# RWKV outputs in two sweeps of a bank, and larger steps of attention, scan and filters, in a two-layer encoder

## The chip, the cores and the metric

The kernel runs on one core of one Trainium2 chip. The metric is the device time of one execution in microseconds (us). Three runs of the kernel before took 3458.44, 3468.43 and 3473.36 us; their median is 3468.43.

## What is computed

A trunk of two layers on 1024 tokens with 1024 channels, all in float32. Each layer normalises, mixes tokens, adds, normalises again and applies a SwiGLU block; shifts, scales and gates come from a condition vector. Layer 1 mixes with long convolutions whose filters are computed from positions. Layer 0, where the change lies, mixes with two groups side by side:

```
y_attn = blocked_gqa(q, k, v)                # 8 heads of 64, 2 heads of keys, softmax over all 1024 keys
state = state * w_t + sz * b_t + v_t * k_t   # RWKV-7, 8 heads of 64 x 64, sz = state z_t
y_t   = state r_t                            # one scan forward, one backward, summed
...
return concat(y_attn, groupnorm(y) + bonus, gated) @ w_out
```

The filters of layer 1 depend on weights alone (`hid @ w_out`, a decay window, then a transform), so they can be computed at any time before layer 1.

## The kernel before

**Storage.** SBUF is cut into pages of 128 x 1024 floats and PSUM into its eight banks. Both are handed out and taken back while the program is written down, the oldest free one first. In the mixer's second part the banks are in two groups of four: group 0 for RWKV, group 1 for attention and the filters.

**The work of layer 0's mixer.** First come the projections (`stream`), with the start of the first RWKV unit beside them (`first`). Then comes a loop over the RWKV units, `for i in range(1, len(units) + 2)` in `mixer`. A unit is a direction and a pair of heads; there are eight, and each goes through three stages in three successive turns of the loop:

- `rwkv_x`: decays by a scan (L1214), products inside chunks of 64 tokens (L1263), and inverses of 16 x 16 blocks on VectorE, with trips through DRAM ahead of and behind them.
- `rwkv_y`: products of 64 x 64 blocks that make the inverses of whole chunks (L1327), transposes (L1345), the chunk-level products (L1374, L1383, L1393) and their forms by head (L1410).
- `rwkv_s`: what each chunk adds to the state (L1435), 14 steps from state to state (L1452, each followed by one VectorE operation), then the outputs (L1467, L1470) of 16 chunks in two banks, and for the second direction the group norm (`rwkv_post`).

A turn `i` runs `rwkv_s` of unit i-2, `rwkv_y` of unit i-1 and `rwkv_x` of unit i, and beside them a number of steps of `beside()`: attention first, with three steps of the filters' hidden layer in it, then the filters.

**Attention.** A step handles 128 queries of one head against all keys: `scores` (L924, L925, two banks; maxima L928 and L929; exponentials L932), `turn` for the tile before (L947 transposes into two banks one after the other, L948 copies them out), and after each fourth tile `values` (L964), whose bank is held for two pairs of tiles.

**Filters.** `hy_filters` goes over 16 groups of channels; each has four `t`: taps (L1735, windows by exponentials L1737, product L1738) and their transform (L1749, L1698 to L1700), then an eight-point transform on VectorE (`dft8`, L1648 and L1649).

**What sets the order.** Each stage is a Python generator; a `yield` ends a step. `weave` draws steps from several generators in proportion to a length that is given with each: it always takes the next step of the one that has gone through the smallest share of its length. The lengths are the numbers of steps: 27 for `rwkv_s`, 36 for `rwkv_y`, 16 for `rwkv_x`, and 46 to 50 of `beside()`. The framework's scheduler gets the instructions in that order. It may let an instruction that is ready pass one that is not, by its own estimate of times, and then fixes one order for each engine. Pages and banks are bound before that, in the order of the steps.

**Products on TensorE.** The array is used whole or in parts: a product with 64 rows of contraction takes 64 rows of it, one with 64 outputs takes 64 columns. The profile writes this tile as rows\*columns. The outputs alternate, per chunk, between two products over the 128 rows of `UV` (tile 128\*64) and two over a 64-row state (64\*64). A float32 product appears as two MATMUL instructions, so each chunk and line gives four.

Of the kernel before, what the change touches and what calls it, by code (L numbers as in the profile page):

```python
# [32 lines left out]
def rows(ap):  # L33
    """[n*128] (or [a, n*128]) vector -> [rows, 128]."""
    if len(ap.shape) == 2:
        return ap.rearrange("a (r w) -> (a r) w", w=P)
    return ap.rearrange("(r w) -> r w", w=P)
# [9 lines left out]
def weave(*gens):  # L47
    """Runs generators of steps side by side, in proportion to their lengths: (n, generator). A step counts for what it
    yields, or for one; one that yields "wait" has to wait for the others."""
    live = [[0, n, g] for n, g in gens]  # L50
    while live:
        live.sort(key=lambda x: x[0] / x[1])
        s = live[0]
        try:
            cost = next(s[2])
            if cost != "wait":
                s[0] += cost or 1
            elif len(live) > 1:
                s[0] = s[1] * (live[1][0] / live[1][1] + 1e-6)
        except StopIteration:  # L60
            live.pop(0)
# [7 lines left out]
def some(gen, n):  # L69
    """The next n steps of a generator."""  # L70
    for _ in range(n):
        if next(gen, gen) is gen:
            return
        yield


class Kern:
    """The kernel's shared state and building blocks.

    SBUF is cut into pages and PSUM into banks, handed out and taken back while the program is traced: the oldest  # L80
    free one first, so that reuse waits as little as it can. Pages are for float32 ([128, 1040]) or for float32r
    operands of products ([128, 1024]); repage() cuts the free ones anew between the parts of the program.
    """

# [32 lines left out]
    def fence(self, dt, n=1 << 30, first=0):  # L117
        """Only the pages from `first` up to the n-th are for common use."""
# [11 lines left out]
    def repage(self, nf, nr):  # L130
        """Cuts the pages into nf of float32 and nr of float32r; those in use stay."""
# [36 lines left out]
    def set_banks(self, *counts):  # L168
        """Splits the (free) banks into groups."""
# [23 lines left out]
    def small(self, tag, shape, bufs, dt=F32):  # L193
        """One of `bufs` small tiles in turn; the caller sees to it that an older use has ended by then."""
# [20 lines left out]
    def load_cols(self, spec):  # L215
        """spec: list of (key, AP [rows, width] or tuple of APs set side by side); a row becomes a column. Steps of 128."""
# [42 lines left out]
    def split(self, t, shape=(P, 1024)):  # L259
        """The pair of a page, which is given back."""  # L260
# [5 lines left out]
    def load_w(self, ap, kt, ncol):  # L266
        """ap: DRAM [kt*128, ncol] -> (hi, lo), [128, kt, ncol] each; ap may also be what presplit() returned."""
# [9 lines left out]
    def presplit(self, ap, kt, ncol, name):  # L277
        """The pair of load_w() as DRAM tiles."""
# [7 lines left out]
    def mm3(self, ps, w, mov, first=True, last=True, halves=(0, 1)):  # L286
        """ps[n] = sum_k w[k]^T mov[k][:, n-th half]; pairs (hi, lo) of [128, M] and [128, 1024]. The first and last
        addends may be left to other calls."""
# [9 lines left out]
    def proj_steps(self, w, c0, width, h, g=0, ahead=None, n=4, apart=False):  # L298
        """proj_tile() in n steps; the halves one after the other if `apart`."""
# [15 lines left out]
    def stream(self, w, h, tiles, g=0):  # L315
        """Projections one after another, each one's `post` beside the next: (column, width, post), post(banks) a generator."""
# [19 lines left out]
    def proj_tile(self, w, c0, width, h, g=0, ahead=None):  # L336
        """w[:, c0:c0+width]^T h in two banks; a column in `ahead` is that of the next call, whose weights are loaded here."""
# [33 lines left out]
    def ada_first(self):  # L371
        """Layer 0's first two sixths, by the tensor engine."""
# [19 lines left out]
    def ada_cols(self, layer, part, half, acc, g):  # L392
        """The columns of half a sixth from rows to be summed."""
# [13 lines left out]
    def ada_part(self, layer, part, g=0, lag=0):  # L407
        """Modulation columns of one sixth: [128, 8] at self.mod[:, layer*48 + part*8]. The last product of a half comes
        `lag` steps after its sums."""
# [35 lines left out]
    def rstd(self, acc, n):  # L445
        """1/sqrt(mean_D(x^2) + eps) on all partitions, [128, 512] of a half in PSUM; acc holds sums of squares."""
# [12 lines left out]
    def normed(self, xT, steps, use, lag, keep=None):  # L459
        """use(n, m, r) for the halves n of the tiles m of x, r the bank of rstd(); `steps` yields (n, m) as they get done,  # L460
        half 0 first. A tile that is done goes to the tile `keep` in DRAM. Half 0 is used beside the steps of half 1, from
        its step `lag` on."""
# [31 lines left out]
    def inv_sqrt(self, out, ps, mult, add=None, floor=None):  # L494
        """out = 1/sqrt(ps*mult + add) or 1/sqrt(max(ps, floor))."""
# [8 lines left out]
    def norm_h(self, xT, layer, which, steps, lag, keep=None):  # L504
        """rmsnorm(x)*gain*(1+scale)+shift as pairs of [128 channels, 1024 tokens]; for the rest see normed()."""
# [23 lines left out]
    def head_cols(self, sq, g):  # L529
        """sq [128 = 2 heads x 64, 1024 tokens] -> bank [128 tokens, 8 blocks, 2 heads] of sums."""  # L530
# [5 lines left out]
    def head_bcast(self, cols, n, g):  # L536
        """cols [128 tokens, 8, 2 heads] -> bank [128 = 2 heads x 64, 512] of token half n."""
# [7 lines left out]
    def to_tok(self, out, src, g):  # L545
        """src [128 channels, 1024 tokens] -> out [128 tokens, 8 blocks, 128 channels]."""
# [9 lines left out]
    # The up-projections multiply blocks of 2 x 2 (two tiles of outputs, halves of the channels, halves of the tokens)  # L556
    # with seven products, Winograd's form of Strassen's: with C = A B,
    # S1 = A21 + A22, S2 = S1 - A11, S3 = A11 - A21, S4 = A12 - S2,
    # T1 = B12 - B11, T2 = B22 - T1, T3 = B22 - B12, T4 = T2 - B21,
    # U2 = A11 B11 + S2 T2, U3 = U2 + S3 T3,  # L560
    # C11 = A11 B11 + A12 B21, C12 = U2 + S1 T1 + S4 B22, C21 = U3 - A22 T4, C22 = U3 + S1 T1.

    def ffn(self, xT, before, layer, up=iter(()), down=iter(()), low=None):
        """x, in pages once the steps `before` are done -> pages of x + the FFN's part and the last steps to them; `up` and
        `down` run beside the two halves. These steps use few of the first `low` pages for operands."""
# [62 lines left out]
        # the first pair of tiles: plain products, while the sums are made  # L628
# [38 lines left out]
        def prep():  # L667
            """The left operands, in the order of the products."""
# [72 lines left out]
        # down, the last tiles first  # L741
# [27 lines left out]
    def matvec_add(self, xT, w, ys, layer, part, g=0, keep=None):  # L769
        """x += gate * (w^T y); x is given as pages, or as tiles in DRAM, which are updated or else kept as pages."""  # L770
# [26 lines left out]
    def matvec_halves(self, xT, w, ys, layer, part, low=None):  # L797
        """matvec_add() by halves of the tokens: loads the weights and returns steps that yield (half, tile); ys are given back."""
# [27 lines left out]
    def attn_tiles(self):  # L826
        """Keys, queries and token-major values, kept in DRAM: what becomes of each projection, for stream()."""
# [6 lines left out]
        def normed(gain, keep):  # L834
            """RMSNorm over the head and rotary positions."""
# [46 lines left out]
    def attention(self, out, G):  # L882
        """Softmax attention with queries on partitions; fills out[0..3] with DRAM tiles [128 channels, 1024 tokens]."""
# [5 lines left out]
        def keys(g):  # L889
            """[hi; hi] and [lo; lo] of a group's keys."""  # L890
# [9 lines left out]
        def queries(t):  # L900
            """The queries of a pair of heads: [hi; lo] and [lo; hi]."""
# [8 lines left out]
        def scores(t, qt, e):  # L910
            """Products with all keys, maximum, exponentials and their sum: a page [128 queries, 1024 keys]."""
# [27 lines left out]
        def turn(pr, t, qt, e):  # L939
            """Keys on partitions, two tiles of queries side by side: pages [128 keys, 4 tiles, 256 queries]."""  # L940
            if qt % 2 == 0:
                st["p", e] = [self.page((P, 4, 256)) for _ in range(2)]
            for n in range(2):
# [6 lines left out]
                yield  # L950
            self.free(pr)

        def values(t, qt):
            """Sums of the values, [2 heads x 64, 256 queries up to tile qt]."""
# [7 lines left out]
            for k in range(8):  # L962
                for e in range(2):
                    nc.tensor.matmul(o[H64[e], x : x + 256], v[:, k, H64[g]], pT[e][k // 4][:, k % 4], start=k == 0, stop=k == 7)  # L964
                if k % 2 == 1:
                    yield
            self.free(pT)
            if qt % 4 == 3:
# [12 lines left out]
                yield  # L981
# [7 lines left out]
        for i in range(n + 1):  # L989
            if i < n:  # L990
                exps[i] = scores(*steps[i])
                yield
            if i:
                yield from turn(exps.pop(i - 1), *steps[i - 1])
            if i % 4 == 0 and i:
                yield from values(*steps[i - 1][:2])
        self.free(st["k"], v)

# [30 lines left out]
    def padded(self, ps, width=P):  # L1029
        """Two banks -> page [width, 1026] with a zero before and after; gives the banks back."""  # L1030
# [9 lines left out]
    def mixed(self, pad, j, width=P):  # L1040
        """The centred token shift of projection columns 768 + 128 j.., given padded: page."""
# [9 lines left out]
    def rwkv_tiles(self):  # L1051
        """What becomes of each projection of this part, for stream(): decay rates, in-context rates and output gates of all
        heads; r, k, v, -kk, bonus and token-major v of the pairs of heads; all kept in DRAM."""
# [3 lines left out]
        def rates(key, j, b0, dst):  # L1057
            def post(ps):
# [5 lines left out]
                # a direction's values as [hi; lo] ([lo; hi] for the second); the weights' hi on both halves, lo beside the values' hi  # L1064
# [136 lines left out]
    # A unit is a direction and a pair of heads; c = 2 pr + p is a chunk of 64 tokens, e a head of the pair. In a tile of  # L1201
# [895 lines left out]
def consts():  # L2097
    """Arrays that depend on the shapes alone."""
    f = np.float32
    k = {}  # L2100
# [76 lines left out]
```

## Time and profile before

| what | value |
| --- | --- |
| median of three runs | 3468.43 us |
| span of the profiled execution | 3477.4 us |
| time of the profiled execution itself | not recorded apart from its span |
| instructions | 52810 |
| the mixer's second part (the loop), from 440 to 1345 us | 905 us |
| turns of the loop that hold attention and all three stages | 94 to 108 us each |
| mean granted TensorE clock over the span | 0.956 |

The span runs from the first to the last instruction of one profiled execution. Shares of busy time are shares of that span. Products are pipelined and overlap on TensorE, so the distance from one start to the next says more than their lengths.

### The profile page before, as it was taken

The numbers are of one execution on the slowest core, as the hardware profiler recorded it, in microseconds if no ns is written. First come the engines' busy times: TensorE is split into PE (matmuls) and PEld (weight loads), VectorE is DVE, ScalarE is ACT, GpSimd is POOL, SyncE is SP. The second block draws the span as 40 slices with busy tenths as digits, with TensorE's granted clock in tenths as the row PEclk, the third lists the DMA queues.
The fourth block names the chain that finished last, engine by engine and source line by source line (L and its number), as shares of the span: only waits on it lengthen the run. The fifth ranks groups of instructions, "written<-read, shape, count | busy, mean of one in ns | idle before, by whom it ended". The sixth has DMA issues, their size and how long they took to land.

```text
span 3477.4 us, 52810 instructions
## 1 busy us (share of the span) xinstructions
PE 3277.4 (94%) x20739; PEld 2639.1 (76%) x20739; DVE 2355.9 (68%) x4281; ACT 1255.1 (36%) x2296; POOL 240.6 (7%) x502
## 2 busy tenths in 40 slices
PE   8999989999998998999999999989987799999998
PEld 4577766777677887887788887778876688888887
DVE  5345556566667778587777666589987786667545
ACT  4523245556543543342223333321221153333211
POOL 2000000000011231000000220000000000000000
PEclk9789989999998999999999999999998899999999
DMA  7454523333324326234444994324336523223411
GB/s 261 172 164 148 159 84 75 73 96 82 73 63 105 99 77 213 79 127 151 158 147 135 359 356 160 103 81 144 121 104 228 177 74 108 73 73 129 146 53 49
DMA packets 332536, 458.89 MB, mean 132 GB/s; under 512 B 103992, under 2 KB 234897, under 8 KB 332288
## 3 DMA queue, kind: packets, MB, share of 16 engines
q1 hardware_dynamic: 292576, 321.65, 30.1%
q0 software_dynamic: 39536, 133.81, 11.3%
q8 instruction: 163, 2.67, 0.3%
q14 instruction: 85, 0.70, 0.1%
q10 hardware_dynamic: 176, 0.07, 0.0%
HBM read 311.27 MB, written 141.56 MB: 130 GB/s over the span
## 4 chain that ended last, share of the span: by engine, by line
PE 60%; DVE 9%; DMA 5%; issue 4%; ACT 2%; SPq 0%; POOL 0%; DVEq 0%; ACTq 0%; POOLq 0%
PE bk L296 22%; PE bk L600 7%; PE bk L602 7%; PE bk L601 7%; PE bk L1749 4%; PE bk L1735 2%; PE bk L1770 2%; DMA p<-in_ada_w_dram 2%; DVE p L1648 1%; DVE p L257 1%; PE bk L1263 1%; PE bk L1327 1%; PE bk L947 1%; DMA p<-in_hy_w_in_dram 1%; PE bk L964 1%
## 5 line engine op out<-in xcount | busy, mean ns | idle before, releaser
L296 PE MATMUL bk<-p,p 128*128 128x512 f32 (+1 forms) x5136 | 1252.3, 403 | 66.9 <-ACT p L256 26.4
L296 PEld LDWEIGHTS bk<-p,p 128*128 128x128 f32 (+1 forms) x5136 | 979.5, 193 | 304.4 <-ACT p L256 30.1
L256 ACT ACTIVATE p<-p 128x512 fp32r<-128x512 f32 (+3 forms) x534 | 395.8, 759 | 930.3 <-PE bk L601 260.6
L257 DVE TENSOR_TENSOR p<-p,p 128x512 fp32r<-128x512 f32 (+3 forms) x534 | 443.5, 848 | 225.3 <-ACT p L256 183.6
L601 PE MATMUL bk<-p,p 128*128 128x512 f32 x1248 | 488.3, 392 | 3.8 <-DVE p L257 3.8
L600 PE MATMUL bk<-p,p 128*128 128x512 f32 x1248 | 488.4, 393 | 0.0
L602 PE MATMUL bk<-p,p 128*128 128x512 f32 x1248 | 487.6, 392 | 0.2 <-DVE p L257 0.2
L601 PEld LDWEIGHTS bk<-p,p 128*128 128x128 f32 x1248 | 236.3, 189 | 53.4 <-DVE p L257 4.7
L602 PEld LDWEIGHTS bk<-p,p 128*128 128x128 f32 x1248 | 236.2, 189 | 50.4 <-DVE p L257 0.8
L600 PEld LDWEIGHTS bk<-p,p 128*128 128x128 f32 x1248 | 236.1, 189 | 48.9
L787 DVE SCALAR_TENSOR_TENSOR p<-bk,mod,p 128x512 f32<-128x512 f32 x192 | 135.0, 745 | 119.8 <-PE bk L296 116.6
L1648 DVE TENSOR_TENSOR p<-p 128x128 f32<-128x128 f32 (+2 forms) x544 | 174.0, 383 | 0.0
L429 DVE SCALAR_TENSOR_TENSOR p<-p,cond,p 128x512 f32<-128x512 f32 x140 | 104.5, 748 | 82.7 <-DMA p<-in_ada_w_dram 81.0
L1749 PE MATMUL bk<-p,p 128*128 128x128 f32 x1024 | 137.0, 290 | 2.7 <-DVE p L1700 2.6
L1749 PEld LDWEIGHTS bk<-p,p 128*128 128x128 f32 x1024 | 126.5, 201 | 7.9 <-ACT p L1737 2.4
L928 DVE TENSOR_REDUCE mx<-bk 128x1 f32<-128x512 f32 x128 | 86.9, 685 | 61.8 <-PE bk L925 58.8
L1737 ACT ACTIVATE p<-delta,k_tneg 128x128 f32<-128x128 f32 x256 | 87.9, 394 | 84.0 <-DMA hs<-p 14.0
L1036 ACT COPY p<-bk 128x512 f32<-128x512 f32 (+1 forms) x80 | 44.0, 589 | 197.3 <-DVE p L1797 64.3
L948 ACT COPY p<-bk 128x512 f32<-128x512 f32 x128 | 74.4, 588 | 105.3 <-PE bk L947 100.7
L932 ACT ACTIVATE p<-bk,mx 128x512 f32<-128x512 f32 x128 | 87.0, 686 | 29.4 <-DVE mx L929 29.0
L947 PE MATMUL bk<-k_ident,p 128*128 128x128 f32 x512 | 85.0, 294 | 10.8 <-ACT p L932 9.3
L1327 PEld LDWEIGHTS bk<-p,p 64*64 64x64 f32 x2048 | 73.0, 137 | 28.9 <-issue 17.6
(404 smaller groups left out, 4373.4 us busy)
## 6 DMA issues: line engine op xcount, KB each, us to landing
p<-in_ffn_w_dram SPq DMA_DIRECT2D x120, 512.0 KB, 4.5
p<-in_ada_w_dram SPq DMA_DIRECT2D x96, 512.0 KB, 4.5
sp_f<-p POOLq DMA_DIRECT2D x36, 512.0 KB, 5.5
p<-sp_f POOLq DMA_DIRECT2D x36, 512.0 KB, 5.4
hs<-p POOLq DMA_DIRECT2D x64, 256.0 KB, 3.1
p<-hs SPq DMA_DIRECT2D x32, 512.0 KB, 4.2
p<-sp_r SPq DMA_DIRECT2D x24, 512.0 KB, 5.6
p<-sp_x SPq DMA_DIRECT2D x24, 512.0 KB, 4.5
```

The lines of the kernel that those rows point to most:

```text
L256: self.nc.scalar.activation(out=hi, in_=src, func=AF.Copy)
L257: self.nc.vector.tensor_tensor(out=lo, in0=src, in1=hi.bitcast(F32), op=ALU.subtract)
L296: nc.tensor.matmul(ps[n], a, b[:, HALVES[n]], start=s, stop=e)
L429: nc.vector.scalar_tensor_tensor(out=acc, in0=wt[:, i], scalar=self.cond[:, k : k + 1], in1=acc, op0=ALU.mult, op1=ALU.add)
L600: nc.tensor.matmul(ps, op[:, 0, k], mh, start=start and k == 0, stop=False)
L601: nc.tensor.matmul(ps, op[:, 0, k], ml, start=False, stop=False)
L602: nc.tensor.matmul(ps, op[:, 1, k], mh, start=False, stop=stop and k == 3)
L787: nc.vector.scalar_tensor_tensor(out=xs, in0=ps[n], scalar=self.modc(layer, part, m), in1=xs, op0=ALU.mult, op1=ALU.add)
L947: nc.tensor.transpose(pt[:, j], pr[:, k * P : (k + 1) * P], self.ident)
L1327: nc.tensor.matmul(pt[H[p], pr], lhs(e, pr, p), rhs[H[p], 8 * e + pr], start=True, stop=True)
L1648: tt = lambda o, a, b, op: nc.vector.tensor_tensor(out=o, in0=a, in1=b, op=op)
L1749: nc.tensor.matmul(ps[:, j, ri], F[2 * d + t2 // 4][:, t2 % 4, 128 * ri : 128 * ri + 128], tp[:, j, d], start=d == 0, stop=d == 1)
```

## The change

Two things. First, in `rwkv_s` the outputs of a bank are made in two sweeps: all products with `UV` (the very first of them marked as the start), then all products with the states (the last one marked as the end). Second, many `yield`s go. Attention has one per step, the blocks of `rwkv_y` and `rwkv_x` one per bank, the sums of `rwkv_s` one per bank, and a filter step now holds the transform of `t` with the taps of `t + 1` written ahead of it. The lengths for `weave` are set to the new numbers of steps. `rwkv_x` in `first()` also has 12 steps in place of 16, while its length there stays at 30. Arithmetic, operands, tiles and transfers stay. The diff also takes out comments.

```diff
 def turn(pr, t, qt, e):
                 self.fbank(pt)
-                yield
             self.free(pr)
 def values(t, qt):
-                if k % 2 == 1:
-                    yield
...
                 self.fbank(o, rb)
-                yield
...
             if i < n:
                 exps[i] = scores(*steps[i])
-                yield
             if i:
-                yield from turn(exps.pop(i - 1), *steps[i - 1])
+                turn(exps.pop(i - 1), *steps[i - 1])
             if i % 4 == 0 and i:
-                yield from values(*steps[i - 1][:2])
+                values(*steps[i - 1][:2])
+            yield
 def rwkv_x(self, u, G):
-                if j == 1:
-                    yield
 def rwkv_y(self, u, G):
-                    if pr == 3:
-                        yield
...
                 nc.scalar.copy(BT[i][:, q : q + 4], pt)
                 self.fbank(pt)
-                yield
+            yield
...
             nc.scalar.copy(ZV[:, :, :, 0:64], pt)
             self.fbank(pt)
-            yield
...
-                    if pr == 3:
-                        yield
 def rwkv_s(self, u, ys, out, G):
-                if c == 3:
-                    yield
...
             for j in range(8):
                 c = 8 * i + j
-                only = c == order[0]
                 for e in range(2):
-                    nc.tensor.matmul(pt[H[e], j], UV[i][:, j, e], R[e][:, c], start=True, stop=only)
-                if not only:
-                    for e in range(2):
-                        nc.tensor.matmul(pt[H[e], j], S[H[e], c], RP[H[e], c % 2, c // 2], start=False, stop=True)
-                if j % 2 and j < 7:
-                    yield
+                    nc.tensor.matmul(pt[H[e], j], UV[i][:, j, e], R[e][:, c], start=j == 0, stop=False)
+            later = [j for j in range(8) if 8 * i + j != order[0]]
+            for j in later:
+                c = 8 * i + j
+                for e in range(2):
+                    nc.tensor.matmul(pt[H[e], j], S[H[e], c], RP[H[e], c % 2, c // 2], start=False, stop=j == later[-1])
 def mixer(self, w, h, ada):
-                if n in (210, 230, 250):
+                if n in (50, 55, 60):
                     next(f)
...
-            n = (0, 48, 48, 48, 48, 50, 48, 46, 50, 48)[i]
+            n = (0, 12, 12, 12, 12, 12, 16, 33, 33, 33)[i]
             gens = [(n, some(other, n))]
             if i > 1:
-                gens.append((27, self.rwkv_s(units[i - 2], ys, outr, 0)))
+                gens.append((19, self.rwkv_s(units[i - 2], ys, outr, 0)))
             if i <= len(units):
-                gens.append((36, self.rwkv_y(units[i - 1], 0)))
+                gens.append((20, self.rwkv_y(units[i - 1], 0)))
             if i < len(units):
-                gens.append((16, self.rwkv_x(units[i], 0)))
+                gens.append((12, self.rwkv_x(units[i], 0)))
 def hy_filters(self, g):
-                for t in range(4):
+                def taps(t):
...
-                    yield
+                    return tp
+                nxt = taps(0)
+                for t in range(4):
+                    tp = nxt
+                    if t < 3:
+                        nxt = taps(t + 1)
                     ps = self.bank(g, (P, 2, 2, W))
```

## The prediction

> **What bounds the kernel now.** I read the whole span first, then stretches of it, then the order of TensorE's products inside the stretch that the change touches. The page of the profile gives the span and TensorE's share.
>
> ```profile
> span 3477.4 us, 52810 instructions
> PE 3277.4 (94%) x20739; PEld 2639.1 (76%) x20739; DVE 2355.9 (68%) x4281; ACT 1255.1 (36%) x2296; POOL 240.6 (7%) x502
> PE 60%; DVE 9%; DMA 5%; issue 4%; ACT 2%; SPq 0%; POOL 0%; DVEq 0%; ACTq 0%; POOLq 0%
> ```
>
> The chain that ended last is 60% TensorE. The 3477.4 us are the span of the profiled execution; the three runs without a profile have a median of 3468.43 us, so the profiled execution lies 9 us (0.3%) above it. What I work out are differences, and I take them off the median. A measurement of this kernel can tell about 0.5% (17 us) from no change.
>
> The changed steps lie in one stretch, from 440 to 1345 us. In the view by windows the columns are the length, then the busy time of PE, PEld, DVE, ACT and POOL, the granted clock, DMA share and GB/s.
>
> ```profile
> 440.00:1345.00 905.00, 855.13 (x9870) 683.91 (x9869) 606.03 (x1554) 469.76 (x1133) 99.84 (x168) 0.95 0.34 87
> 836.00:940.00 104.00, 101.85 (x1208) 71.46 (x1208) 72.32 (x157) 63.33 (x135) 3.01 (x6) 1.00 0.38 88
> 1048.00:1165.00 117.00, 105.34 (x1151) 90.44 (x1148) 80.92 (x236) 51.49 (x139) 22.15 (x36) 0.90 0.35 88
> 1258.00:1345.00 87.00, 85.88 (x721) 77.49 (x720) 75.54 (x241) 31.38 (x94) 23.33 (x36) 1.00 0.43 133
> 1345.00:1362.00 17.00, 6.49 (x49) 5.91 (x50) 13.00 (x37) 7.62 (x8) 4.51 (x6) 0.61 0.74 267
> ```
>
> The last four rows are three of the nine turns of the mixer's loop (one unit's start, one unit's middle and one unit's end, beside attention or filters) and what follows. TensorE is busy for 98% of the turn at 836 and for 99% of that at 1258, DVE for 70% and 87%. So here TensorE's own time sets the pace, and I ask what that time consists of. In the timeline of TensorE the columns are start, length to the last end, operation, tile of the array (rows\*columns), shape of the moving operand, and how many products.
>
> ```profile
> 1332.76 3.81 PE L1749 MATMUL bk<-p,p 128*128 128x128 f32 x32 [0.34 <-DVE p L1700]
> 1336.50 0.33 PE L1470 MATMUL bk<-p,p 64*64 64x64 f32 x4
> 1336.76 0.34 PE L1467 MATMUL bk<-p,p 128*64 128x64 f32 x4
> ...
> 1340.19 0.33 PE L1470 MATMUL bk<-p,p 64*64 64x64 f32 x4
> ...
> 1184.01 0.71 PE L1749 MATMUL bk<-p,p 128*128 128x128 f32 x4
> 1184.65 0.33 PE L1452 MATMUL bk<-p,p 64*64 64x64 f32 x4
> 1184.91 0.44 PE L1345 MATMUL bk<-k_ident,p 128*128 128x128 f32 x2
> 1185.28 1.61 PE L1327 MATMUL bk<-p,p 64*64 64x64 f32 x48
> 1186.73 0.28 PE L1452 MATMUL bk<-p,p 64*64 64x64 f32 x4
> 1186.85 0.63 PE L1327 MATMUL bk<-p,p 64*64 64x64 f32 x16
> 1187.41 0.44 PE L1345 MATMUL bk<-k_ident,p 128*128 128x128 f32 x2
> ```
>
> Between 1336.50 and 1340.19 the two lines of the outputs alternate in groups of four, 14 groups in 3.69 us, 0.264 us each. From 1185.28 to 1187.41 there are 68 products of the same 64x64 size, of two lines but of one tile, in 2.13 us. The row in their midst, L1452, costs nothing extra, although it is another line into another bank: 1186.85 - 1186.73 = 0.12 us for four. At 1184.65 the same four products, with 128\*128 ahead and behind, take 0.26. So it is the change of tile that costs: 0.26 - 0.12 = 0.14 us. With that one change taken off, a product in a run is (2.13 - 0.14) / 68 = 0.029 us. A wide tile pays about as much: four of L1749 from 1184.01 to 1184.65 take 0.64 us, against 4 x 3.74 / 32 = 0.47 in the run of 32 at 1332.76. I take 0.14 for every change, with 0.10 and 0.17 as bounds.
>
> How often does it occur? I counted, over the timeline of TensorE from 440 us (first row below) to 1345 (last row), how many products have another tile than the one ahead of them: 950 of 9869. At 0.14 that is 133 of 905 us.
>
> ```profile
> 439.83 0.61 PE L296 MATMUL bk<-p,p 128*128 128x512 f32 x2
> ...
> 1343.20 1.02 PE L1492 MATMUL bk<-p,k_blkones 128*128 128x512 f32 x2
> ```
>
> Does the order come from the code or from the scheduler? I wrote out the turns of `weave` with the tile of each step's products: 959 changes in the order in which the code hands its steps over, against 950 on the chip. By turn of the loop it is 122 to 126 for the second to fifth turn, and the chip has 113 to 143. So the scheduler keeps to the code's order nearly everywhere, and the new order can be written out too.
>
> **The outputs in two sweeps.** The rows of the two lines in the stretch (busy time, mean ns):
>
> ```profile
> L1467 PE MATMUL bk<-p,p 128*64 128x64 f32 x512 | 45.2, 244 | 0.0
> L1470 PE MATMUL bk<-p,p 64*64 64x64 f32 x480 | 41.4, 242 | 0.0
> ```
>
> These 992 products stand in 248 groups of four, 248 x 0.264 = 65.5 us. After, a bank has 32 products of one tile and then 28 to 32 of the other: 992 x 0.029 = 28.8 us, and 16 banks with a change in their middle and mostly one at the end, 32 x 0.14 = 4.5. That is 32 us less. As some groups already ran on into products of the same tile (my list has 242 changes behind these two lines, not 248), I take 31. The flags of the first and last product are not an operation; the number of products, copies and additions stays.
>
> **Larger steps.** A turn of the loop had 48 + 27 + 36 + 16 = 127 steps and has 12 + 19 + 20 + 12 = 63. Attention yields once per tile of queries and no more after scores, each four transposes and each four products of the values; `rwkv_y` and `rwkv_x` yield per bank, no longer per half bank; a filter step holds the products of L1749 and the next L1735. The list of turns, changes behind the products of each part, before and after: attention 208 and 68; `rwkv_y` 238 and 114; `rwkv_x` 56 and 28; states (L1452) 93 and 53; additions to the state (L1435) 24 and 15; filters 90 and 45; the rest 8 and 8. Outside the outputs that is 717 and 331, 386 fewer, x 0.14 = 54 us (39 to 66 by the bounds). In all 85 us.
>
> **What is given back.** First, the four banks of attention. `scores` takes two; `turn` for the tile before takes one after the other; the values hold a fourth for half of the time. With three in the ring the second `turn` gets a bank that `scores` has just filled, and has to wait for its maximum and exponentials. That stood apart by other steps before, and is in one step now. It is so in 32 of the 64 steps, and 8 more times the bank of the values itself is such a one. The length of the wait, with empty queues, is two maxima, the scaling and one exponential:
>
> ```profile
> L928 DVE TENSOR_REDUCE mx<-bk 128x1 f32<-128x512 f32 x128 | 86.9, 685 | 61.8 <-PE bk L925 58.8 <-ACT p L1269 2.5
> L929 DVE TENSOR_SCALAR mx<-mx 128x1 f32<-128x1 f32 x64 | 13.3, 209 | 0.9
> L932 ACT ACTIVATE p<-bk,mx 128x512 f32<-128x512 f32 x128 | 87.0, 686 | 29.4 <-DVE mx L929 29.0
> L947 PE MATMUL bk<-k_ident,p 128*128 128x128 f32 x512 | 85.0, 294 | 10.8 <-ACT p L932 9.3 <-DVE p L979 0.8 <-ACT p L948 0.6
> ```
>
> 2 x 0.685 + 0.209 + 0.686 = 2.3 us, less 0.5 for four transposes that run meanwhile, 1.8 us. Queued behind the waiting transposes on TensorE are the values and whatever RWKV step follows. I expect the scheduler to put RWKV steps of the 4 x 1 us or so that lie between two attention steps into the gap; then each of the 40 costs two changes of tile, 80 x 0.14 = 11 us. The bound on the other side is a rival below.
>
> Second, the turn of the loop gets shorter than one unit's start is long. Its first scan is at 643.63, and the first products that need its result are at 747.51:
>
> ```profile
> 643.63 2.32 DVE L1214 TENSOR_TENSOR_SCAN p<-p,p 128x1040 f32<-128x1040 f32 x1 [1.07 <-DMA p<-sp_w]
> ...
> 747.51 1.15 PE L1327 MATMUL bk<-p,p 64*64 64x64 f32 x32
> ```
>
> 104 us, a turn of the loop as it is now. If turns shorten by 9 us, `rwkv_y` starts that much later in its turn, and only attention and the states can fill. TensorE is not busy for 905 - 855 = 50 us of the stretch now. Between nothing and 9 us for each of eight units lies 0 to 72; most of the 98% busy turns speak for the low end, and I take 15.
>
> Third, the end: from 1345 to 1362 DVE is busy for 13 of 17 us and TensorE for 6.5, so the filters' tail is DVE's already. There the last turn's 41 fewer changes (6 us) buy half: 3 us given back. The taps made one step ahead save a wait that hardly exists, 2.7 and 0.4 us in all (last column), so I cost them at nothing.
>
> ```profile
> L1749 PE MATMUL bk<-p,p 128*128 128x128 f32 x1024 | 137.0, 290 | 2.7 <-DVE p L1700 2.6
> L1735 PE MATMUL bk<-wo,p 128*128 128x256 f32 x256 | 80.1, 446 | 0.4 <-DVE p L1738 0.3
> ```
>
> The start of unit 0, beside the projections, has 12 steps instead of 16 at the same weight, and ends earlier; the wait of L1327 for it is 4.3 us once:
>
> ```profile
> PE bk L1327 <- DMA p<-o: 4.3, 1, 4.3
> ```
>
> That is 0 to 4 us gained; I leave it at nothing. No queue of SP or POOL gets more to do; the loads and stores move along with their steps.
>
> The sum: 31 + 54 - 11 - 15 - 3 = 56 us. 3468 - 56 = 3412 us. With 0.10 and 0.17 per change and 0 to 40 for the unit's start it runs from 3385 to 3438.
>
> **Rivals.** *The scheduler cuts the pieces anew* (the change doesn't do what it says). A step that is not ready is passed by others, and each passing makes changes of tile again. Against it stands 959 against 950. For it, the steps are longer and wait oftener. Then the outputs keep their 31, the other 54 shrink to half, and the losses stay: 3468 - (31 + 27 - 29) = 3439 us.
>
> *DVE and ACT become the bound.* DVE is at 70% of the turn at 836, 69% of that at 1048, and 87% of the last. If it can hold no more than 75%, those turns may shrink to 96, 108 and not at all, where I expect about 95, 108 and 81: some 10 us less gain, 3422 us. The Trainium skill says in "TensorEngine Tiling (Array Packing)", PSUM Bottleneck, that packing speeds up TensorE but not the emptying of PSUM, which may then become the bound; by that the gain would be cut in every turn, and the trace shows room for it in all but the last.
>
> *The unit's start paces the loop.* If a turn cannot get shorter than the 104 us of scan to result, only the two turns without such a start gain: 99 - 40 and 68 - 27 changes, 100 x 0.14 = 14 us, 3454 us, no change that can be told. Against it: L1327 waits for that result once.
>
> *Slower: TensorE waits inside the attention step.* The place is the second `turn` (and the first product of the values), 40 times. If nothing stands in the gap and the queues of DVE and ACT hold other work, a wait is 1.8 us and as much again, 3.6 x 40 = 144 us, against 85 gained; the two other losses (18 us) come on top. 3468 - 85 + 144 + 18 = 3545 at that price; it decides from 40 waits of (85 - 18) / 40 = 1.7 us on, so already the bare 1.8 us with no filling ends at 3473, and 2.5 us at 3501, which I take. For it: one order holds for all engines, and a wait misjudged at compile time stalls everything behind it. Against it: L947 waits 9.3 us for L932 in 512 products now. The Trainium skill, "TensorE: Matmul & The Clock Gate", HAM oscillation, adds that an idle gap above about 3.4 us halves TensorE's clock; the turn at 1048, with 12 us not busy, has 0.90 granted, which agrees.
>
> **How the numbers follow.** Forecast 3412 us, chance 0.60. Pieces cut anew 0.15, DVE and ACT 0.07: both faster by over 0.5%. The unit's start 0.10: within 0.5%. The wait in attention 0.08: slower. So faster 0.82, same 0.10, slower 0.08. The range from 3385 to 3458 takes in the forecast's own, the first three rivals, and leaves out the slower one and the tails, 0.16.
>
> **What would show it.** In the timeline of TensorE after: L1467 and L1470 in runs of 28 to 32, 0.9 to 1.1 us each; 400 to 480 changes of tile in the stretch; the stretch from the first L924 to the last L1749 some 55 us shorter, its turns at 90 to 95 us; TensorE still above 93% busy there, DVE up by 5 points. Wrong would be: over 600 changes (cut anew), L947 waiting for L932 for more than 40 us (the slower rival), L1327 waiting for the reloaded inverse for more than 30 us (the unit's start), or DVE above 85% in the turns with attention.

## The result and the profile after

The changed kernel takes 3483.53 us in the median of 20 runs (3461.60 to 3498.55), the kernel before 3473.53 in as many runs on the same chip (3458.44 to 3482.30). The ratio is 1.0027 [1.0016, 1.0038]: no change that can be told at 0.5%, where I forecast 3412 us. The head of the page of the profiled execution after, then its chain of waits by engine:

```profile
span 3480.2 us, 52831 instructions
PE 3244.6 (93%) x20739; PEld 2630.9 (76%) x20739; DVE 2349.4 (68%) x4281; ACT 1253.5 (36%) x2296; POOL 241.4 (7%) x502
PE 67%; DVE 14%; DMA 9%; issue 5%; ACT 4%; SPq 0%; POOL 0%; DVEq 0%; ACTq 0%; POOLq 0%
```

TensorE is busy 33 us less than before and the span is 3 us longer. So work went away, and other time came in its place. The chain's row doesn't say which: the one before adds up to 80% of its span, since that chain can be followed back only to 660 us, and the one after to 99%, so their shares can't be compared. The groups of the two output lines and two waiting lines after, from the view by lines:

```profile
L947 PE MATMUL bk<-k_ident,p 128*128 128x128 f32 x512 | 87.0, 299 | 13.2 <-ACT p L932 13.2
...
L1439 PE MATMUL bk<-p,p 64*64 64x64 f32 x448 | 39.8, 242 | 11.3 <-DVE p L1288 5.7 <-DVE p L1440 5.5
...
L1454 PE MATMUL bk<-p,p 128*64 128x64 f32 x512 | 23.2, 233 | 0.0
...
L1459 PE MATMUL bk<-p,p 64*64 64x64 f32 x480 | 21.0, 233 | 0.0
```

L1454 and L1459 are the old L1467 and L1470: 44.2 us of busy time in place of 86.6. L1439 is the old L1452, the products from state to state; it now waits 11.3 us. What a turn looks like, in TensorE's timeline after:

```profile
701.56 0.66 PE L947 MATMUL bk<-k_ident,p 128*128 128x128 f32 x4
702.15 0.27 PE L1374 MATMUL bk<-p,p 64*64 64x64 f32 x1
702.15 0.27 PE L1439 MATMUL bk<-p,p 64*64 64x64 f32 x2
...
702.42 0.65 PE L963 MATMUL bk<-p,p 128*64 128x256 f32 x2
702.99 0.33 PE L1439 MATMUL bk<-p,p 64*64 64x64 f32 x4
703.25 0.66 PE L947 MATMUL bk<-k_ident,p 128*128 128x128 f32 x4
703.84 1.96 PE L1384 MATMUL bk<-p,p 64*64 64x128 f32 x32
709.04 0.27 PE L1439 MATMUL bk<-p,p 64*64 64x64 f32 x2 [3.23 <-DVE p L1288]
...
713.63 1.03 PE L1454 MATMUL bk<-p,p 128*64 128x64 f32 x26
```

The sweep at 713.63 runs through. But attention's two L947 groups, handed over as one step, stand apart with four changes of tile from one to the other, and at 705.8 TensorE stops for 3.2 us: L1439 needs its state from VectorE's L1440. VectorE is idle then, as its own timeline shows:

```profile
708.63 0.16 DVE L1286 TENSOR_TENSOR p<-p 128x1 f32<-128x1 f32 x1 [5.78 <-DMA p<-g]
708.71 0.28 DVE L1440 SCALAR_TENSOR_TENSOR p<-bk,DC,p 128x64 f32<-128x64 f32 x1
```

L1286 is the first operation of the next unit's inverses in `rwkv_x`. It waits 5.78 us for its blocks to come back from DRAM (`g`), and in the order that was fixed for VectorE it stands ahead of L1440, whose product had long been there (L1439 at 702.99). From 440 to 1345 us I count 633 changes of tile after against 950 before; the written order of the loop has 353 (e8 below).

### The profile page after: what moved, and what is told of

Its sections match the earlier page's. It is cut to its first block, busy times and chain, and to the rows that moved or that the text cites. A ratio compares the mean times of both kernels' runs of the same rounds, so it can differ in the third digit from the quotient of the medians.

```text
span 3480.2 us, 52831 instructions
## 1 busy us (share of the span) xinstructions
PE 3244.6 (93%) x20739; PEld 2630.9 (76%) x20739; DVE 2349.4 (68%) x4281; ACT 1253.5 (36%) x2296; POOL 241.4 (7%) x502
## 4 chain that ended last, share of the span: by engine, by line
PE 67%; DVE 14%; DMA 9%; issue 5%; ACT 4%; SPq 0%; POOL 0%; DVEq 0%; ACTq 0%; POOLq 0%
PE bk L296 28%; PE bk L601 6%; PE bk L600 6%; PE bk L602 6%; PE bk L1743 3%; DMA p<-in_ada_w_dram 2%; DVE p L257 2%; DVE p L1635 2%; PE bk L1764 2%; PE bk L1321 2%; PE bk L963 1%; PE bk L1723 1%; PE bk L947 1%; PE bk L1259 1%; DMA p<-in_ffn_w_dram 1%
## 5 line engine op out<-in xcount | busy, mean ns | idle before, releaser
L932 ACT ACTIVATE p<-bk,mx 128x512 f32<-128x512 f32 x128 | 87.0, 686 | 48.2 <-DVE mx L929 37.8
L947 PE MATMUL bk<-k_ident,p 128*128 128x128 f32 x512 | 87.0, 299 | 13.2 <-ACT p L932 13.2
L1321 PE MATMUL bk<-p,p 64*64 64x64 f32 x2048 | 89.8, 236 | 9.7 <-DVE p L1353 4.9
```

Of the source, the lines that this page charges most:

```text
L947: nc.tensor.transpose(pt[:, j], pr[:, k * P : (k + 1) * P], self.ident)
L1321: nc.tensor.matmul(pt[H[p], pr], lhs(e, pr, p), rhs[H[p], 8 * e + pr], start=True, stop=True)
```

## Where the time went: work, waits and the clock

I split the loop, from the projections' last product to the filters' last, into time in which TensorE has nothing under way (idle), what the halved clock costs at most (half of the busy time that falls into stretches granted at half speed), and the rest, its work at full clock. Each row of the table is one profiled execution. The length and the busy time are one row of the view by windows; of before, then of after, then of the sweeps alone (e1):

```profile
450.00:1343.00 893.00, 843.91 (x9793) 675.07 (x9792) 598.87 (x1541) 468.79 (x1131) 99.84 (x168) 0.95 0.33 86
```

```profile
455.00:1336.00 881.00, 803.61 (x9789) 660.21 (x9789) 591.26 (x1533) 466.92 (x1131) 99.71 (x167) 0.94 0.33 88
```

```profile
446.00:1312.00 866.00, 811.39 (x9787) 658.08 (x9786) 594.25 (x1541) 466.73 (x1129) 99.20 (x166) 0.95 0.34 88
```

Idle is 893 - 843.9 = 49 us before and 881 - 803.6 = 77 after. The same for every kernel that ran (us; e8 is told apart):

| kernel | loop | idle | gaps over 1 us: number, sum | clock at most | work |
| --- | --- | --- | --- | --- | --- |
| before | 893 | 49 | 11, 34 | 35 | 809 |
| before, start at 34 (e16), at 40 (e6) | 886, 908 | 40, 56 | 11, 28; 15, 41 | 38, 41 | 807, 811 |
| finer alternation (e3) | 963 | 45 | 11, 34 | 61 | 858 |
| two sweeps alone (e1) | 866 | 55 | 15, 42 | 32 | 779 |
| sweeps + filters (e11) | 858 | 53 | 14, 37 | 29 | 776 |
| larger steps alone (e2), at old pace (e5) | 886, 893 | 64, 67 | 20, 43; 22, 50 | 27, 36 | 796, 790 |
| sweeps + attention (e9) | 876 | 69 | 20, 57 | 36 | 772 |
| sweeps + RWKV (e10) | 883 | 71 | 23, 58 | 40 | 773 |
| sweeps + sums + filters (e12) | 865 | 61 | 20, 48 | 28 | 776 |
| after | 881 | 77 | 26, 58 | 50 | 754 |
| after, start at 18 (e7), 20 (e13) | 890, 894 | 76, 77 | 21, 56; 26, 58 | 54, 49 | 760, 768 |
| after, start at 22 (e4), 24 (e14), 26 (e15) | 872, 894, 880 | 75, 86, 75 | 25, 58; 24, 63; 24, 58 | 39, 45, 44 | 758, 763, 761 |

Two things part cleanly. The sweeps take 30 us of work and leave the idle time within what it is in the kernels before (40 to 56). Every kernel with larger steps of attention, RWKV or the sums has 20 to 26 gaps above 1 us; every kernel without has 11 to 15. From the two kernels with the sweeps and no larger steps but the filters' (e1, e11) to the six with all of the change, the means go: work 777.5 to 761 (17 less), idle 54 to 78 (24 more), clock 31 to 47 (16 more).

One source of the idle time parts the kernels just as cleanly. These are VectorE's waits in the loop for the reloaded blocks `g`, of before (L1292 there is the new L1286), then of after (in all, times, longest):

```profile
DVE p L1292 <- DMA p<-g: 11.1, 4, 4.9
```

```profile
DVE p L1286 <- DMA p<-g: 26.7, 7, 5.8
```

Before, none of TensorE's idle time falls into these waits; after, 7.7 us do. In the nine kernels with larger steps of all of RWKV (e2, e4, e5, e7, e10, e13 to e15, after) it is 5 to 11 us, in e9 2 us, and in the seven others at most 0.6. In the mean of the six kernels with all of the change it is 8 of the 24 us. There it can go as at 705.8: an operation that waits for its reload stands in VectorE's order ahead of one that TensorE needs.

## How waits cost clock

A gap of TensorE in the trace after, as four windows of one period of the clock record, 3.41 us each:

```profile
1118.88:1122.29 3.41, 2.76 (x40) 2.15 (x41) 1.95 (x6) 3.33 (x11) 2.45 (x3) 1.00 0.56 111
1122.29:1125.71 3.42, 0.24 (x4) 0.10 (x4) 0.62 (x2) 1.30 (x4) 1.09 (x3) 1.00 0.54 113
1125.71:1129.12 3.41, 3.22 (x15) 3.22 (x16) 2.24 (x14) 0.80 (x2) 0.51 (x1) 0.51 0.00 0
1129.12:1132.53 3.41, 3.41 (x27) 3.22 (x27) 2.35 (x8) 2.49 (x7) 0.00 (x0) 0.99 0.00 0
```

The third number from the end is the granted clock. A window in which TensorE was busy for 0.24 us is followed by one at half the clock, although there is then work for nearly all of it; here the clock is back after that one window. Between 440 and 1340 us of 17 traces (all but e8), of the windows at full clock that were busy for under 40%, 118 of 118 were followed by half clock; of those at 40 to 50%, 41 of 49; at 50 to 60%, 34 of 78; at 90% and more, 28 of 3308. So a wait that leaves a window under 40% busy is paid a second time: the next 3.41 us do at most half their work, which is up to 1.7 us by estimate. The Trainium skill, "TensorE: Matmul & The Clock Gate", HAM oscillation, puts the limit at idle gaps above about 3.4 us; in 35 of the 118 windows no single wait reached 2.5 us, and all 35 were followed by half clock; the measurement decides.

It shows in the runs too. In the 20 runs of the changed kernel the order is the same and the clock goes from 0.945 to 0.957; time and clock correlate at -0.88; this doesn't part cause from effect, as an execution that waits more has a lower clock too. Span times mean clock is 3327 us before and 3307 after, 20 less; but the mean clock is 0.958 before and 0.950 after, and 0.008 of 3480 are 28 us, which is what it can have cost at most.

## The experiments

All ratios are to the kernel before, run on the same chip.

**e1, the sweeps alone:** only the last hunk of `rwkv_s`, with the lengths for 21 steps.

```diff
-                gens.append((27, self.rwkv_s(units[i - 2], ys, outr, 0)))
+                gens.append((21, self.rwkv_s(units[i - 2], ys, outr, 0)))
```

> The kernel before, with the outputs of a bank in two sweeps and nothing else (a bank is one step, 21 steps of rwkv_s in place of 27). The compiled order has 745 changes of tile on TensorE in the loop against 940. Theory A (a change of tile costs 0.14 us wherever it goes, and the larger steps are what loses): 195 x 0.14 = 27 us less in the loop, some of it lost at the start of the next part; 0.993 to 0.996 of the time before. Theory B (the loop's length does not reach the end: what follows waits for its weights and pages anyway): no change, 0.998 to 1.002.

3454.01 us, 0.9942 [0.9924, 0.9961]. The work of the loop falls by 30 us, as forecast (31), and 20 us reach the end. TensorE's time does set the pace.

**e2, the larger steps alone:** all other hunks; the outputs keep alternating, in one step a bank.

```diff
-                if j % 2 and j < 7:
-                    yield
```

> The changed kernel with the outputs alternating as before (one step a bank): all the larger steps, no sweeps. The compiled order has 854 changes of tile against 940 before and 625 in the changed kernel. Theory A: 86 x 0.14 = 12 us won against some 35 us of new waits of TensorE and 5 us at the loop's start, so 1.006 to 1.010 of the time before. Theory B: 0.999 to 1.003, as the changed kernel has.

3472.62 us, 0.9992 [0.9979, 1.0005]. The order that the scheduler fixes has 854 changes against 940 before: 86 fewer, not 386. The work falls by 13 us, the idle time rises by 15. The ratio lies in the range of theory B.

**e3, more changes of tile:** the outputs alternate by head.

```diff
                 for e in range(2):
                     nc.tensor.matmul(pt[H[e], j], UV[i][:, j, e], R[e][:, c], start=True, stop=only)
-                if not only:
-                    for e in range(2):
+                    if not only:
                         nc.tensor.matmul(pt[H[e], j], S[H[e], c], RP[H[e], c % 2, c // 2], start=False, stop=True)
```

> The kernel before with the outputs alternating by head: one product of either kind in turn, groups of two instructions in place of four. 1167 changes of tile against 940. Theory A: each group of four takes 0.31 us in place of 0.264, 248 x 0.046 = 11 us at the least, and 227 x 0.14 = 32 us at the most: 1.003 to 1.009. Theory B: within 0.2% of the time before.

3550.00 us, 1.0219 [1.0187, 1.0250], more than either theory expected: its loop has 49 us more work for 227 more changes, 0.22 us each. Its timeline of TensorE:

```profile
1395.39 0.33 PE L1469 MATMUL bk<-p,p 64*64 64x64 f32 x2
1395.65 0.33 PE L1467 MATMUL bk<-p,p 128*64 128x64 f32 x2
1395.91 0.32 PE L1469 MATMUL bk<-p,p 64*64 64x64 f32 x2
...
1402.29 0.47 PE L1469 MATMUL bk<-p,p 64*64 64x64 f32 x2
1402.69 0.47 PE L1467 MATMUL bk<-p,p 128*64 128x64 f32 x2
```

A group of two takes 0.26 us, as long as a group of four before (0.264). So in such a short alternation a group costs the same with two products as with four, and halving the groups doubles the price. My 0.14 on top of 0.029 a product would have made it 0.20.

**e4 and e7, the changed kernel with another pace of the first unit's start** (22, which ends the 12 steps where the 16 ended before; and 18):

```diff
-        weave((250, self.stream(w, h, tiles)), (60, ada(1)), (30, first()))
+        weave((250, self.stream(w, h, tiles)), (60, ada(1)), (22, first()))
```

> The changed kernel with length 22 in place of 30 for the first unit's start, so that its 12 steps keep the pace of the 16 before. Theory A with a loss at the start: the loop begins some 5 us earlier than in the changed kernel, and the time falls by 3 to 6 us against it: 1.001 of the time before. Without such a loss: 1.003, as the changed kernel.

> The changed kernel with length 18 for the first unit's start (pace 12/18; e4 had 12/22, the changed kernel 12/30). 646 changes of tile. Theory C: the first unit's start falls behind the projections, 0.990 to 0.995, no worse than e4 unless the loop's first product waits for it. Theory D: a lot of its own, 0.990 to 1.004.

e4: 3449.80 us, 0.9921 [0.9900, 0.9942]; e7: 3460.82 us, 0.9965 [0.9951, 0.9979]. e4 was expected at 1.001 to 1.003 by either theory, and is far below. One number that moves 12 steps beside the projections is worth 1%, some 35 us, and 18 isn't better than 22.

**e5, e2 at length 22; e6, the kernel before at length 40:**

> The larger steps alone (no sweeps), with length 22 for the first unit's start: 858 changes of tile in the loop, 82 fewer than before. Theory C (what the changed kernel lost, it lost by the pace of the first unit's start, which went from 16/30 to 12/30): as e4 won 27 us over the kernel before and the sweeps alone 20, the rest of 7 us belongs to the larger steps, 0.998, and 3 us less than e2. Theory D (the pace matters only by shifting which page and bank goes to whom, so that each kernel gets a lot of its own of up to 20 us): anything from 0.992 to 1.004, with no order by pace.

> The kernel before with length 40 in place of 30 for the first unit's start, so that its 16 steps get the pace that the changed kernel has (16/40 = 12/30). 961 changes of tile. Theory C: the loss of the changed kernel against e4, 0.8 to 1%, comes back here: 1.006 to 1.010, some 5 us of it ahead of the loop. Theory D: within 0.4% of the time before, either way.

e5: 3471.33 us, 0.9992 [0.9983, 1.0001], as e2. e6: 3493.36 us, 1.0054 [1.0042, 1.0066]. e5 lies above theory C, which asked for 0.998 and 3 us less than e2, and inside the wide range of theory D; e6 lies just below theory C, 1.006 to 1.010, and above the 0.4% of theory D. The pace acts in one kernel and not in the other.

**e8, the changed kernel in its written order:**

```diff
-    with tile.TileContext(nc, schedule_with_timeline_sim=True) as tc:
+    with tile.TileContext(nc, schedule_with_timeline_sim=True, linearize=True) as tc:
```

> The changed kernel with the framework told to keep the written order on every engine (all phases, not the loop alone). 353 changes of tile in the loop, close to the 350 of the list of turns. If the price of a change is 0.14 us, TensorE saves another 38 us in the loop; but in one fixed written order every wait that the scheduler would have filled stands open: the 40 waits of attention at 1.8 us and more, and those of the other parts of the program. I expect the loop 50 to 200 us longer than in the changed kernel, and the whole 1.05 or more.

13215.17 us, 3.8045 [3.7979, 3.8110], clock 0.623. This order has the 353 changes of tile that I had written out, and the largest wait of TensorE is

```profile
PE bk L600 <- DVE p L257: 1573.9, 276, 62.4
```

It fixes one order across all engines, which is more than I wanted, and shows no more than that the kernel lives on the scheduler's reordering. In the changed kernel the written order, with 353 changes, was not the one that ran, with 633.

**e9, e10, e11: the sweeps with one kind of larger step each** (attention; `rwkv_x`, `rwkv_y` and the sums, at length 22; filters). The edits are the hunks of the change for these functions, with their lengths.

> Of the larger steps only those of attention, on top of the two sweeps; filters, sums and the blocks of RWKV stay in small steps. Compiled changes of tile in the loop 711 (two sweeps alone 745, the changed kernel 633). In the runs so far, span times granted clock was 3327 us for the kernel before, 3307 for the changed kernel, 3303 with two sweeps alone; the mean clock 0.958, 0.950 and 0.957. Theory A (TensorE's new waits come with the larger steps of attention): it is idle for 65 to 77 us in the loop as in the changed kernel (49 with two sweeps alone), the clock falls to 0.950 to 0.953, ratio 0.998 to 1.003. Theory B (they come with the larger steps of RWKV): idle near 50 us, clock 0.957, the 34 changes fewer count, ratio 0.991 to 0.994. Theory C (only all of it together makes the waits): the same as B here and in the two other runs.

> Of the larger steps only those of RWKV (blocks of rwkv_x and rwkv_y per bank, sums per bank), on top of the two sweeps, with the first unit's start at length 22, the pace of before; attention and filters stay in small steps. Compiled changes of tile in the loop 700 (two sweeps alone 745). Theory A (waits by attention): idle near 50 us in the loop, clock 0.957, 45 changes at 0.14 us are 6 us less than two sweeps alone, ratio 0.990 to 0.993. Theory B (waits by RWKV): idle 65 to 77 us, clock 0.950 to 0.953, ratio 0.998 to 1.003. Theory C (only all together): as A here.

> Of the larger steps only those of the filters, on top of the two sweeps; attention and RWKV stay in small steps. Compiled changes of tile in the loop 727 (two sweeps alone 745). All three theories: idle near 50 us in the loop, 18 changes at 0.14 us are 2.5 us less than two sweeps alone, ratio 0.991 to 0.994. If the filters' larger steps are what makes the waits, the last three turns (from 1040 us on) have over 10 us more idle than with two sweeps alone and the ratio is 0.996 or more.

e9: 3463.38 us, 0.9969 [0.9953, 0.9985]; e10: 3463.43 us, 0.9969 [0.9957, 0.9982]; e11: 3445.90 us, 0.9921 [0.9901, 0.9942]. None of the three theories holds alone: attention and RWKV each add some 15 us of idle to the sweeps, the filters none. The waits of TensorE in the loop with the largest sums, of e9 and then of e10 (in all, times, longest):

```profile
PE bk L924 <- ACT p L932: 14.8, 9, 3.4
PE bk L924 <- ACT p L894: 9.9, 1, 9.9
PE bk L1323 <- ACT p L1332: 6.2, 1, 6.2
```

```profile
PE bk L1443 <- DVE p L1444: 17.6, 10, 4.1
PE bk L947 <- ACT p L932: 9.2, 4, 6.7
```

Each waits in its own place: with attention's larger steps the scores (L924) wait for a bank that the exponentials (L932) hold, with RWKV's the next state's product (L1443) waits for VectorE's step ahead of it (L1444). In the sweeps alone these were 4.8 and 1.5 us. Of the 17.6 us, 10 are three waits between 1065 and 1076 us, where VectorE has no idle time and L1444 stands behind the filters' L1638 and the next unit's work.

**e12, sweeps, sums and filters:**

```diff
-                if c == 3:
-                    yield
```

> Two sweeps, larger steps of the filters and of the state's sums (one step a bank); the blocks of rwkv_x and rwkv_y and attention stay in small steps. It parts the waits seen with RWKV's larger steps (58 us in gaps of TensorE above 1 us, with 17.6 us of L1443, the products from state to state, waiting for VectorE's L1444) between the blocks and the sums. Compiled changes of tile in the loop 715 (two sweeps and filters 727). If the blocks bring the waits: gaps above 1 us sum to 35 to 45 us in the loop, 12 changes at 0.14 us are 2 us less than two sweeps with filters, ratio 0.990 to 0.993. If the sums bring them: gaps above 1 us of 50 us or more, ratio 0.995 or more.

3462.19 us, 0.9968 [0.9955, 0.9980]; 20 gaps of 48 us in all. By the ratio that was expected the sums bring waits; the gaps lie between the two bounds. But TensorE's waits for the states are 6.1 us in all (L1450 for L1451; 3.1 in e11), and larger ones lie where this edit touches nothing: 9.6 and 9.0 us in attention (13.0 and 4.9 in e11) and 7.5 us in the group norm (L533 for L1493; none in e11). An edit of two lines draws the whole order anew, so a difference of 0.5% can't be laid to the lines edited.

**e13 to e16, other lengths of the first unit's start** (20, 24 and 26 in the changed kernel, 34 in the kernel before):

> The changed kernel with length 20 for the first unit's start (30 in it, 22 is the pace of before). Known ratios: 0.9965 at 18, 0.9921 at 22, 1.0027 at 30. Theory P (only the pace acts, with its best near 22): between 0.992 and 0.9965. Theory L (each compiled order is a lot): anywhere from 0.989 to 1.004, off the line through its neighbours by over 0.003 here or in the two other lengths.

> The changed kernel with length 24 for the first unit's start. Theory P: 0.992 to 0.996, on the line from 0.9921 at 22 to 1.0027 at 30 (0.9948). Theory L: off that line by over 0.003 here or at 26.

> The changed kernel with length 26 for the first unit's start. Theory P: 0.995 to 1.000, on the line from 22 to 30 (0.9974). Theory L: off that line by over 0.003 here or at 24.

> The kernel before with length 34 for the first unit's start (30 in it, 1.0054 at 40). Theory P: 1.000 to 1.004, on the line (1.002). Theory L: off the line by over 0.003 somewhere among the four runs; here anything from 0.996 to 1.008.

3472.61 us, 0.9996 [0.9983, 1.0009]; 3467.73 us, 0.9979 [0.9962, 0.9996]; 3466.34 us, 0.9984 [0.9970, 0.9999]; and 3470.14 us, 0.9982 [0.9967, 0.9998]. From 18 to 30 the changed kernel has 0.9965, 0.9996, 0.9921, 0.9979, 0.9984, 1.0027; at 20 it lies 0.005 off the line through its neighbours. Three of the four lie outside what theory P allowed (only 26 is inside), so theory L holds: each order is a lot of its own, with a standard deviation of 0.0035 (12 us) around a mean of 0.9979. The changed kernel drew the worst of the six.

## Why the prediction was wrong

**The bound** was right for the sweeps: of the 30 and 33 us of work that e1 and e11 took off TensorE, 20 and 27 reached the end. DVE is busy 591 us of the loop after and 599 before, and was no bound over the loop; but its order holds TensorE up for some us at a time, behind a reload or behind the filters (e10), and the prediction's sum had no term for that.

**The price of a change** was right in size: the sweeps 31 us forecast, 30 of work measured; the larger steps take off 112 changes more than the sweeps (745 and 633 in the order that the scheduler fixes), 16 us at 0.14, and 17 us of work went. It isn't a constant: in groups of two (e3) a change costs 0.22.

**The step that failed** is "So the scheduler keeps to the code's order nearly everywhere, and the new order can be written out too." 959 and 950 agreed as counts; that doesn't make the orders the same. With larger steps the scheduler cut them anew: 633 changes on the chip against 353 written, where I expected 400 to 480 and had named 600 as the sign of this rival. So 54 us became 17. How far the order before was the written one is not shown.

**What is given back** was mis-sized. I had 11 + 15 + 3 = 29 us, part of it for attention's 40 waits, which the scheduler was to fill. Measured are 24 us of idle time in many places, no one of them large (L947 for L932 went from 9.3 to 13.2 us, far from the 40 of the slower rival; L1321, the old L1327, waits for the reloaded inverse 3.2; 8 in the mean fall into VectorE's waits for its reload), and up to 16 us of clock, which I had in the slower rival alone and not in the sum. For the rival "cut anew" I gave 3439: the mean of the six orders is 0.9979 x 3468 = 3461 us, 22 above it. Its own terms, against those measured, give as much: 10 by the larger steps (17 for 27), 1 by the sweeps and up to 16 by the clock, less 5 by the idle time (24 for 29). That this agrees to the microsecond is chance. The bounds of the sum were added up with terms left out: 3385 without the tail's 3 us, 3438 without the tail's 3 and attention's 8; with them they are 3388 and 3449.

**The first unit's start**, costed at nothing, is one of the things that redraw the order; it has no price that the runs show beyond the lot.

**The tail** was no gain in this order: from the filters' last product to the first of the FFN it is 116 us after, 110 before, and 102 to 109 in the other five orders of the changed kernel. With 5 us more ahead of the loop, 12 less in it and 4 more behind the tail, this makes the 3 us by which the two spans differ; the medians of 20 runs differ by 10, as single executions vary.

The sum with what was measured, for the mean of the six orders: 30 less by the sweeps and 17 by the larger steps, 24 of idle time and up to 16 of clock against it, so 7 us gained in the loop; the six loops are 885 us in the mean, 8 less than before. The spans of the six are 3465 us in the mean, 12 less than before. That of the changed kernel lies 15 us above this mean: 8 in the tail, 4 ahead of the loop, 6 behind the tail, and 3 less in the loop. Why a given order waits where it does stays open beyond the reloads; so does what part of the 16 us the clock really took, since no run sets the clock by itself. That larger steps of attention, RWKV or the sums bring waits over 1 us is shown by eleven kernels with them against six without.

Two versions came out lowest: the sweeps with the larger filter steps and all else small (3445.90 us, 0.9921) and the changed kernel at length 22 (3449.80 us, 0.9921). The first keeps its few gaps; the second has 25, and is the lucky end of its six.

## What to carry to other kernels

Take from the code's order only what need not wait: products that stand ready, such as a bank's two sweeps, gain by standing together; work that waits on other engines was better left in small steps here, which the scheduler can put into gaps. Look at what stands ahead of the needed operation on the other engine too: there an operation that waits for a transfer holds up all behind it. Count in the order that is fixed for the engine, not in the one that the code hands over. Before laying half a per cent to an edit, move something that should not matter and see how far the time goes by itself.

## What was not expected of the hardware

A window of 3.41 us that was under 40% busy was followed by TensorE's half clock in 118 of 118 cases; it needs no idle window. The clock doesn't always come back after one busy window: of 345 windows at half clock that were busy for 90% and more, 113 were followed by another. And alternating groups of two and of four float32 products of 64 columns cost the same 0.26 us at full clock; at a granted clock of 0.50 (e3, from 1400.6 us) a group of two takes 0.40, so not all of that price follows the clock.
